# S5 input side by pairs of tiles, thinner scan steps and a shorter way to the output side in a two-layer encoder kernel

## The chip, the cores and the metric

The kernel runs on one core of one Trainium2 chip. The metric is the device time of one execution in microseconds (us), as the median of several runs. All data are fp32, and all weights lie in HBM when the program starts.

Engines are called as in the profile: PE is TensorE's matmul, PEld its weight load, DVE VectorE, ACT ScalarE, POOL GpSimd, SP SyncE (it issues most of the DMAs; SPq is its queue). An `x16` behind an instruction in the trace is a count of records. A matmul of plain fp32 operands leaves two records, so eight such instructions are `x16`; the transposes (a matmul against the identity) and the matmuls on fp32r operands leave one.

## The reference

A sequence of 256 frames of width 2048 passes two layers. Each has its own modulation from a conditioning vector, a mixer on a width of 4096, and a residual with LayerNorm. Layer 0 is a gated linear attention, layer 1 a state-space model (S5):

```
mod = silu(c) @ ada_w + ada_b                  # shift, scale, gate per layer
u   = x * (1 + scale) + shift
h   = gla_mixer(u)  or  s5_mixer(u)
x   = layer_norm(alpha * x + (1 + gate) * h)

def s5_mixer(u_in):
    u, z = split(u_in @ w_in)                  # 2048 -> 4096 + 4096
    # per group of 16 channels, 64 complex states, 256 groups:
    x_t = lambda * x_{t-1} + B u_t             # lambda = exp(dt * a)
    y_t = Re(C x_t) + d * u_t
    y   = gelu(y)
    y   = y * sigmoid(y @ w_glu + b_glu)       # 4096 x 4096
    return (y * silu(z)) @ w_out               # 4096 -> 2048
```

## The kernel before, in words

**Weight streams.** Nearly all the time goes into products with large fp32 weights. A weight is read in tiles of 128x1024, which hold two blocks of 128 rows (`kp` counts such pairs) and 512 columns (a group `g`). `wload` (L133) loads one; its buffer comes from `ring`, a list of buffers that is used in rotation: four of the pool `w`, and, while a phase has memory to spare, some of the phase's own pool, which are put at the head of the list. `split` makes two fp32r tiles of it: `hi`, a cast on ACT (L109), and `lo`, the weight minus `hi`, on DVE (L110). There are three buffers for each. PE then makes three products, hi x hi, hi x lo, lo x hi: `st_step` (L168 to L170) has 24 matmuls of 128x256 per weight tile, into four PSUM banks of the pool `mm` (five banks). Another PSUM pool, `ax`, has three banks and serves all that is not a weight stream.

**The S5 layer** runs in this order: `su`, 8 groups of 8 tiles, the input projection u; `sz`, 8 groups, the gate z; `gl`, the 4096x4096 GLU product; `op`, the output projection. In the trace of before su runs from 777.2 to 1052.3 us, sz to 1324.8, gl to 1692. The state-space model is computed beside su and sz, in pieces that are put between two weight tiles. Its 256 groups of channels are handled as 32 tiles `f` of 8 groups; one su group yields four tiles.

**Input side, beside su and the first group of sz.** Time is cut in blocks of 8 frames. For a tile, `b_pow` builds B times powers of lambda, `wb` (one copy on ACT, three operations on DVE, from `rb`, loaded for two tiles at a time), `b_tr` transposes it (pswb, two banks one after the other, each copied to `wbt` by ACT), `s_in` turns u into blocks (a DVE transpose to `vv`, two PE transposes psu, an ACT copy to `U`; it stands behind the last matmul of the group). `s_mm` multiplies: 8 instructions `pss<-wbt,U`, whose result is transposed on DVE into the block states `sx`, and 8 instructions `pss<-wb,rb`, whose result is copied to `kT` on ACT. `k_out` transposes kT (psk), copies it to `ks` on ACT, adds d on the diagonal (`dm` and `ks` on DVE) and writes it to DRAM (`dk`). These pieces stand in the list `bq`; `bstep` takes as many as `b_pace` has run up, 1.5 per weight tile.

**The scan.** `scan` advances the state from block to block, 30 steps for each half of the channels, four small DVE operations a step. The first half is put into the list `bg` behind su's group 4, and `pump` takes `SCAN_RATE` pieces per weight tile.

**Output side, beside sz groups 1 to 7.** When sz's group 0 is done, what is left of `bq` and `bg` is issued, the phase's pool is closed, and another one is opened in the same memory. Per tile `cside` loads `cl` (three DMAs) and `mt` (the matrices from `dk`) and builds C times powers (`wc0`, `wc1`, in `powmul`, L970 and L971, double-buffered); for tiles with f % 8 >= 5 DVE adds the two (L1109). `xstage` transposes the states (xT on DVE, psxs on PE, xS on ACT), and `ystage` multiplies: `psy<-mt,U` and `psy<-wc,xS`, once for each wc. The second half of the scan, three steps per tile, runs in the same list, and `pump` takes 2.311 pieces per weight tile.

**What sets the order.** The program is written in the order in which these lists are emptied. A scheduler then orders each engine's instructions; pools with few buffers add waits. Each engine works in its own order, and waits on semaphores of the others.

Of the kernel before, what the change touches and what calls it, by code (L numbers as in the profile page):

```python
# [8 lines left out]
F32 = mybir.dt.float32  # L9
# [24 lines left out]
def trunk(ctx, tc, x, c, ln_g, ln_b, ada_w, ada_b, gla_w_in, gla_gate_w2, gla_gate_b, gla_norm_g,  # L34
# [33 lines left out]
    rp.open("rows0")  # L68
    tp = Phase()
# [13 lines left out]
    ones = cp.tile([P, P], F32, name="ones")  # L83
    V.memset(ones, 1.0)
# [18 lines left out]

    last_lo = [None]

    def split(w, name):
        hi = hp.tile([P, 1024], F32R, tag="hi", name="hi" + name)
        lo = lp.tile([P, 1024], F32R, tag="lo", name="lo" + name)
# [5 lines left out]
    ring = [lambda name: wp.tile([P, 1024], F32, tag="w", name=name)] * 4  # L114

    def ring_add(bufs):
        ring[0:0] = bufs

    def ring_tmp(n):
        bufs = [lambda name: tp.tile([P, 1024], F32, tag="wx", name=name, bufs=n)] * n  # L120
        ring_add(bufs)
        return bufs[0]

    def ring_drop(buf):
        ring[:] = [b for b in ring if b is not buf]

    def wload(src, k0, c0, name, last=False):
        if last:
            w = wp.tile([P, 1024], F32, tag="w", name="w" + name)
        else:  # L130
            ring.append(ring.pop(0))
            w = ring[-1]("w" + name)
        dma(w.rearrange("p (k c) -> p k c", k=2),  # L133
            src[k0 * P:(k0 + 2) * P, c0:c0 + 512].rearrange("(k p) c -> p k c", p=P))
        return w

    def split_last(w, name, i):


        hi = (hp.tile([P, 1024], F32R, tag="hi", name="hi" + name) if i % 2 else lp.tile([P, 1024], F32R, tag="lo", name="hi" + name))  # L140
# [256 lines left out]
    early = ring_tmp(2)  # L397
# [9 lines left out]
    l8r = cp.tile([P, 128], F32, name="l8r")  # L407
    l8i = cp.tile([P, 2, 128], F32, name="l8i")
# [32 lines left out]
    def prep_lambda():  # L441
# [301 lines left out]
    ring_drop(early)  # L743
    tp.close()
    tp.open("tmp0b")
    mid = ring_tmp(4)
# [154 lines left out]
    ring_add(spare)  # L901
# [19 lines left out]
    ring_drop(mid)  # L921
    for b in spare:
        ring_drop(b)
# [49 lines left out]
    wu, kts = {}, {}  # L973

    def b_pow(f):
        if f % 2 == 0:
            bload(f // 2)
        a = rb[f // 2][:, f % 2]

        w = tp.tile([P, 8, 16, 8], F32, tag="wu", name=f"wb{f}", bufs=2)  # L980
# [8 lines left out]
        wu[f] = w  # L989

    def b_tr(f):
        wt = tp.tile([P, 8, 128], F32, tag="wbt", name=f"wbt{f}", bufs=2)
        for h in range(2):
            ps = psx(f"pswb{f}{h}")
            for g in range(4):
                PE.transpose(ps[:, g * P:(g + 1) * P], wu[f][:, 4 * h + g].rearrange("p i s -> p (i s)"), ident)
            S.copy(wt[:, 4 * h:4 * h + 4, :], ps.rearrange("p (g r) -> p g r", g=4))
        wb[f] = wt

    def s_in(f, ps):  # L1000
        v = tp.tile([P, 2, 16, 8], F32, tag="vv", name=f"vv{f}", bufs=2)
        V.transpose(v.rearrange("p b i s -> p s b i"), ps[:, :T].rearrange("p (s b i) -> p s b i", s=8, b=2)[:, ::-1])
        pu = psx(f"psu{f}")
        for b in range(2):
            PE.transpose(pu[:, b * P:(b + 1) * P], v[:, b].rearrange("p i s -> p (i s)"), ident)
        U = Ut[f // 8][:, f % 8]
        S.copy(U, pu[:, :T].rearrange("p (b r) -> p b r", b=2))

    def s_mm(f):
        U = Ut[f // 8][:, f % 8]  # L1010
        pss = psx(f"pss{f}")
        for b in range(2):
# [17 lines left out]
    def k_out(f):  # L1030
        kt_ = kts[f]
        pk_ = psx(f"psk{f}")
        for b in range(2):
            PE.transpose(pk_[:, b * P:(b + 1) * P], kt_[:, b], ident)
        pk = pk_[:, :T].rearrange("p (b q i) -> p q b i", b=2, q=4)[:, :, :, :16]
        ks = tp.tile([P, P], F32, tag="ks", name=f"ks{f}", bufs=1)
        S.copy(ks.rearrange("p (q b i) -> p q b i", q=4, b=2), pk)
        dm = tp.tile([16, 8, 16], F32, tag="dm", name=f"dm{f}", bufs=1)
        V.tensor_tensor(dm, ident[:16, :16].unsqueeze(1).to_broadcast([16, 8, 16]),
                        dT[:, 8 * f:8 * f + 8].unsqueeze(2).to_broadcast([16, 8, 16]), op=ALU.mult)  # L1040
        V.tensor_tensor(ks[:16].rearrange("p (q b i) -> p q b i", q=4, b=2), pk[:16],
                        dm.rearrange("p (q b) i -> p q b i", q=4), op=ALU.add)
        kd = dk[16 * f:16 * f + 16, 896:1920].rearrange("i (n c) -> n i c", n=8)
        wdma(kd, ks)
# [285 lines left out]
```

## Time and profile before

| what | us |
|---|---|
| median of 3 runs | 1884.14 |
| lowest and highest run | 1879.79, 1885.82 |
| the profiled execution's own time | 1875.77 |
| its span | 1874.0 |
| PE busy | 1811.6 (97%), 13443 instructions |
| PE weight load busy | 1582.1 (84%) |
| DVE busy | 1441.9 (77%), 2022 instructions |
| ACT busy | 899.1 (48%) |
| POOL busy | 26.9 (1%), 44 instructions |

The mean granted clock of the profiled execution is 0.993. Matmuls are pipelined, so a record's duration (0.28 us for 128x256) is longer than the distance from one start to the next. Costs of PE work are read from the starts. The busy shares are means over stages, so a stage's limit is read from the windows.

### The profile page before, as it was taken

How to read it: one execution, taken by the hardware profiler on the slowest of the kernel's cores; microseconds unless marked ns; L12 is line 12 of the kernel's file. 1: busy time of each engine (PE TensorE's matmuls, PEld its weight loads, DVE VectorE, ACT ScalarE, POOL GpSimd, SP SyncE). 2: the span in 40 equal slices, each digit the busy share in tenths (PEclk: the TensorE clock that was granted, in tenths of full speed). 3: DMA queues.
4: the chain of work that ended last, by engine and by line, in shares of the span. 5: the costliest groups of instructions: out<-in, count | busy, mean ns of one | idle time of the engine just before them, and what ended most of it. 6: DMA issues, size and time to landing. Idle time of an engine off the chain costs nothing.

```text
span 1874.0 us, 33634 instructions
## 1 busy us (share of the span) xinstructions
PE 1811.6 (97%) x13443; PEld 1582.1 (84%) x13443; DVE 1441.9 (77%) x2022; ACT 899.1 (48%) x1259; POOL 26.9 (1%) x44
## 2 busy tenths in 40 slices
PE   6999999999999999999999999999899999999997
PEld 3786797899999888898899889898788888888886
DVE  2787675989999888687799879998767775557556
ACT  3533365655556333654454444554544444444332
POOL 0000000000000000000000000000000000000000
PEclk9999999999999999999999999999999999999999
DMA  9978976789888998564555567898678887668653
GB/s 357 321 256 264 354 246 183 230 284 326 287 290 311 342 346 275 168 178 146 165 154 143 167 202 209 221 255 235 212 250 269 270 267 226 190 190 326 192 172 109
DMA packets 239493, 449.12 MB, mean 240 GB/s; under 512 B 19221, under 2 KB 45263, under 8 KB 238055
## 3 DMA queue, kind: packets, MB, share of 16 engines
q1 hardware_dynamic: 235400, 437.53, 73.2%
q0 software_dynamic: 3168, 8.41, 1.4%
q8 instruction: 105, 1.72, 0.4%
q10 hardware_dynamic: 768, 1.05, 0.2%
q14 instruction: 52, 0.42, 0.1%
HBM read 432.49 MB, written 14.42 MB: 238 GB/s over the span
## 4 chain that ended last, share of the span: by engine, by line
PE 64%; issue 9%; DVE 6%; DMA 6%; ACT 1%; POOL 1%; SPq 0%; DVEq 0%; POOLq 0%; ACTq 0%
PE gl L180 13%; PE gl L181 6%; PE op L157 5%; PE op L155 5%; PE op L156 5%; PE z L170 3%; PE z L168 3%; PE z L169 3%; PE su L168 2%; PE su L170 2%; PE su L169 2%; DMA cl<-rec 2%; PE sz L168 2%; PE sz L170 2%; PE sz L169 2%
## 5 line engine op out<-in xcount | busy, mean ns | idle before, releaser
L110 DVE TENSOR_TENSOR logl<-wgl,higl 128x1024 fp32r<-128x1024 f32 x128 | 156.6, 1224 | 118.7 <-ACT higl L109 113.4
L109 ACT CAST higl<-wgl 128x1024 fp32r<-128x1024 f32 x128 | 134.2, 1050 | 177.9 <-PE gl L180 174.6
L180 PE MATMUL gl<-yp,higl 128*128 128x512 f32 x512 | 181.2, 399 | 3.1 <-ACT higl L109 3.1
L180 PE MATMUL gl<-yb,higl 128*128 128x512 f32 x512 | 178.7, 394 | 0.0
L109 ACT CAST hio<-wo 128x1024 fp32r<-128x1024 f32 x96 | 101.3, 1055 | 155.6 <-PE op L157 131.1
L110 DVE TENSOR_TENSOR loo<-wo,hio 128x1024 fp32r<-128x1024 f32 x96 | 117.3, 1224 | 65.6 <-ACT hio L109 63.6
L280 DVE SCALAR_TENSOR_TENSOR acc<-wa,cs,acc 128x512 f32<-128x512 f32 x215 | 160.7, 747 | 4.0 <-DMA wa<-in_ada_w 1.3
L170 PE MATMUL sz<-u1h,losz 128*128 128x256 f32 x512 | 146.5, 287 | 3.9 <-DVE losz L110 3.9
L168 PE MATMUL sz<-u1h,hisz 128*128 128x256 f32 x512 | 149.8, 293 | 0.2 <-ACT zs L1166 0.2
L168 PE MATMUL su<-u1h,hisu 128*128 128x256 f32 x512 | 149.8, 294 | 0.0
L168 PE MATMUL z<-u0h,hiz 128*128 128x256 f32 x512 | 148.7, 290 | 0.9 <-ACT hiz L109 0.9
L170 PE MATMUL su<-u1h,losu 128*128 128x256 f32 x512 | 147.7, 290 | 0.0
L169 PE MATMUL su<-u1l,hisu 128*128 128x256 f32 x512 | 147.1, 287 | 0.0
L170 PE MATMUL z<-u0h,loz 128*128 128x256 f32 x512 | 145.1, 283 | 1.7 <-DVE loz L110 1.7
L169 PE MATMUL sz<-u1l,hisz 128*128 128x256 f32 x512 | 145.5, 284 | 0.0
L169 PE MATMUL z<-u0l,hiz 128*128 128x256 f32 x512 | 144.7, 283 | 0.0
L181 PE MATMUL gl<-yb,logl 128*128 128x256 f32 x512 | 142.7, 279 | 0.0
L181 PE MATMUL gl<-yp,logl 128*128 128x256 f32 x512 | 141.7, 279 | 0.1
L180 PEld LDWEIGHTS gl<-yp,higl 128*128 128x128 f32 x512 | 95.9, 188 | 27.0 <-ACT higl L109 3.3
L180 PEld LDWEIGHTS gl<-yb,higl 128*128 128x128 f32 x512 | 96.0, 187 | 22.4
L155 PE MATMUL v<-hiv,u0h 128*128 128x512 f32 x256 | 103.3, 410 | 5.2 <-ACT u0h L309 2.6
L109 ACT CAST hiz<-wz 128x1024 fp32r<-128x1024 f32 x64 | 67.1, 1053 | 83.8 <-PE z L169 78.4
(319 smaller groups left out, 4965.8 us busy)
## 6 DMA issues: line engine op xcount, KB each, us to landing
wgl<-in_s_w_glu SPq DMA_DIRECT2D x128, 512.0 KB, 4.7
wa<-in_ada_w SPq DMA_DIRECT2D x115, 512.0 KB, 5.1
a<-in_ada_w SPq DMA_DIRECT2D x32, 1024.0 KB, 11.4
wv<-in_gla_w_in SPq DMA_DIRECT2D x64, 512.0 KB, 6.1
wz<-in_gla_w_in SPq DMA_DIRECT2D x64, 512.0 KB, 5.1
wsu<-in_s_w_in SPq DMA_DIRECT2D x64, 512.0 KB, 3.9
wsz<-in_s_w_in SPq DMA_DIRECT2D x64, 512.0 KB, 5.3
wo<-in_s_w_out SPq DMA_DIRECT2D x64, 512.0 KB, 4.6
```

The costliest lines, as they stand in the source:

```text
L109: S.copy(hi, w)
L110: last_lo[0] = V.tensor_tensor(lo, w, hi.bitcast(F32), op=ALU.subtract).ins
L155: PE.matmul(banks[tt], lhsT=uh, rhs=hi[:, kk, :], start=(k == first), stop=False)
L156: PE.matmul(banks[tt], lhsT=uh, rhs=lo[:, kk, :], start=False, stop=False)
L157: PE.matmul(banks[tt], lhsT=ul, rhs=hi[:, kk, :], start=False, stop=(k == last))
L168: PE.matmul(o, lhsT=wh, rhs=u.hi(k), start=(k == first), stop=False)
L169: PE.matmul(o, lhsT=wh, rhs=u.lo(k), start=False, stop=False)
L170: PE.matmul(o, lhsT=wl, rhs=u.hi(k), start=False, stop=(k == last))
L180: PE.matmul(banks[f], lhsT=hi[:, kk, fs], rhs=u.both(k), start=(k == 0), stop=False)
L181: PE.matmul(banks[f][:, :T], lhsT=lo[:, kk, fs], rhs=u.hi(k), start=False, stop=(k == last))
L280: V.scalar_tensor_tensor(acc[0], w[:, kk, :], cs[:, k:k + 1], acc[0], op0=ALU.mult, op1=ALU.add)
```

## The change

It has six parts.

1. Buffers. `ring` becomes a class, with one ring each for w, hi and lo. Buffers of a phase are appended (used last) where they were put at the head. During su, from its tile (0, 3) on, there is one more w, one more hi and one more lo.
2. Input side by pairs of tiles. u's transposes (psu) of a pair are issued from weight tiles 0 and 3 of the next group, four PE transposes in a row into one bank. `s_mm(p)` has the 32 instructions of two tiles in one piece, in two banks; kT, ks and dm hold a pair each, one buffer. dm and the add to ks go to POOL. `wb` and `wbt` are pairs in the pool `s8`. `b_pace` is 1.0 per weight tile.
3. Scan. Two multiplications become one of twice the size, against a constant `l8` of another layout; four operations become three. `SCAN_RATE` is 1.25.
4. The DVE add of wc0 and wc1 goes; all tiles multiply both.
5. The output side is opened at sz's tile (0, 5), where it was opened behind (0, 7). Two scan steps per tile, not three, and they stand between `cside` and `xstage`. `Y_RATE` is 2.25, and `zs` is allocated group by group.
6. `ones` lies in the phase pool `rows` and not among the constants.

The core of the diff (`b_pow` and `b_tr` change only in that they write into the pair tiles; `...` marks what is left out):

```diff
+    class Ring(list):
+        def take(self, name):
+            self.append(self.pop(0))
+            return self[-1](name)
...
+        def add_tmp(self, tag, dt, n):
+            bufs = [lambda name: tp.tile([P, 1024], dt, tag=tag, name=name, bufs=n)] * n
+            self.extend(bufs)
+            return bufs[0]
-    def ring_add(bufs):
-        ring[0:0] = bufs
...
-    def s_mm(f):
-        U = Ut[f // 8][:, f % 8]
-        pss = psx(f"pss{f}")
...
-        kt_ = tp.tile([P, 2, P], F32, tag="kt", name=f"kT{f}", bufs=2)
+    def s_in2(p, v):
+        pu = psx(f"psu{p}")
+        for i in range(2):
+            for b in range(2):
+                PE.transpose(pu[:, (2 * i + b) * P:(2 * i + b + 1) * P], v[:, i, b].rearrange("p i s -> p (i s)"), ident)
...
+    def s_mm(p):
+        pss = [psx(f"pss{2 * p + i}") for i in range(2)]
+        for i in range(2):
...
+            for b in range(2):
+                for q in range(4):
+                    PE.matmul(pss[i][32 * q:32 * q + 32, b * P:(b + 1) * P], lhsT=U[:, b, 32 * q:32 * q + 32],
+                              rhs=wb[p][:, i, 2 * q + b, :], start=True, stop=True)
+            for b in range(2):
+                for q in range(4):
...
+        kt_ = tp.tile([P, 2, 2, P], F32, tag="kt", name=f"kT{p}", bufs=1)
...
-        dm = tp.tile([16, 8, 16], F32, tag="dm", name=f"dm{f}", bufs=1)
-        V.tensor_tensor(dm, ident[:16, :16].unsqueeze(1).to_broadcast([16, 8, 16]),
...
+        dm = tp.tile([16, 16, 16], F32, tag="dm", name=f"dm{p}", bufs=1)
+        nc.gpsimd.tensor_tensor(dm, ident[:16, :16].unsqueeze(1).to_broadcast([16, 16, 16]),
...
+        nc.gpsimd.tensor_tensor(kv, kv, dm.rearrange("p g i -> p (g i)"), op=ALU.add)
+        for i in range(2):
+            f = 2 * p + i
+            wdma(dk[16 * f:16 * f + 16, 896:1920].rearrange("i (n c) -> n i c", n=8), ks[:, i])
...
-    for f in range(35):
-        if 2 <= f < 34:
-            bq.append(lambda f=f: s_mm(f - 2))
-        if f < 32:
-            bq.append(lambda f=f: (b_pow(f), b_tr(f)))
-        if f >= 3:
-            bq.append(lambda f=f: k_out(f - 3))
+    for p in range(18):
+        if 1 <= p < 17:
+            bq.append(lambda p=p: s_mm(p - 1))
+        for f in (2 * p, 2 * p + 1):
+            if f < 32:
+                bq.append(lambda f=f: (b_pow(f), b_tr(f)))
+        if p >= 2:
+            bq.append(lambda p=p: k_out(p - 2))
...
-        V.tensor_tensor(t1, X, lr.unsqueeze(1).to_broadcast([P, 2, 2, 32]), op=ALU.mult)
-        V.tensor_tensor(t2, X[:, ::-1], li, op=ALU.mult)
-        V.tensor_tensor(t1, t1, t2, op=ALU.add)
-        V.tensor_tensor(N, N, t1, op=ALU.add)
+        V.tensor_tensor(t1, X.unsqueeze(1).to_broadcast([P, 2, 2, 64]), l8[:, h], op=ALU.mult)
+        V.tensor_tensor(t1[:, 0], t1[:, 0], t1[:, 1, ::-1], op=ALU.add)
+        V.tensor_tensor(N, N, t1[:, 0], op=ALU.add)
...
+            if us and kp in (0, 3):
+                us.pop(0)()
+            if (g, kp) == (0, 3):
+                mid = more(1, 1)
...
-        for i in range(4):
-            s_in(4 * g + i, banks[i])
+        for i in range(2):
+            v = s_in(2 * g + i, banks[2 * i:2 * i + 2])
+            us.append(lambda p=2 * g + i, v=v: s_in2(p, v))
...
-        if f % 8 >= SPLIT:
-            V.tensor_tensor(w[0], w[0], w[1], op=ALU.add)
-            w.pop()
...
+    def output_side():
+        bstep(len(bq))
+        while bg:
+            bg.pop(0)()
+        less(mid)
+        tp.close()
+        tp.open("tmp2")
+        sc1 = [lambda cidx=cidx: scan(cidx, 1) for cidx in range(1, 31)]
+        for f in range(34):
+            if f < 32:
+                bg.append(lambda f=f: cside(f))
+            for _ in range(2):
...
+            pump(SCAN_RATE if (g, kp) < (0, 6) else Y_RATE)
+            if (g, kp) == (0, 5):
+                output_side()
```

How the order moves is seen best in the queues themselves. The first place is PE in su's group 3, where tiles 8 and 9 are multiplied. A row gives the line, the operation, out<-in by name, and the size; the digits behind su are group and bank, and those behind pss and wbt the tile, or, after the change, the pair for wbt. Here is the kernel before, for the second tile of the pair alone:

```order
L170 MATMUL su33_8762<-u1h0_7394,losu32_8878 128x256
L1014 MATMUL pss9_8905<-wbt9_8713,U1_7519 32x128 x8
L168 MATMUL su30_8759<-u1h0_7394,hisu33_8927 128x256
L169 MATMUL su30_8759<-u1l0_7396,hisu33_8927 128x256
L170 MATMUL su30_8759<-u1h0_7394,losu33_8928 128x256
L168 MATMUL su30_8759<-u1h0_7394,hisu33_8927 128x256
L169 MATMUL su30_8759<-u1l0_7396,hisu33_8927 128x256
L1024 MATMUL pss9_8905<-wb9_8707,rb4_8595 32x128 x8
L170 MATMUL su30_8759<-u1h0_7394,losu33_8928 128x256
```

And the same place after the change, with both tiles:

```order
L182 MATMUL su33_8681<-u1h0_7394,losu31_8734 128x256
L1038 MATMUL pss8_8761<-wbt4_8612,U1_7519 32x128 x8
L1043 MATMUL pss8_8761<-wb4_8606,rb4_8602 32x128 x8
L1038 MATMUL pss9_8762<-wbt4_8612,U1_7519 32x128 x8
L1043 MATMUL pss9_8762<-wb4_8606,rb4_8602 32x128 x8
L180 MATMUL su30_8678<-u1h0_7394,hisu32_8802 128x256
```

Before, the two halves of a tile stood five su matmuls apart, and tile 8 had its own two pieces some 48 matmuls earlier. Now the four pieces of a pair stand between two su matmuls.

The second place is PE where wb of tile 10 is transposed. Before:

```order
L169 MATMUL su30_8759<-u1l0_7396,hisu32_8877 128x256
L996 MATMUL pswb100_8854<-ident_87,wb10_8847 128x128 x4
L996 MATMUL pswb101_8860<-ident_87,wb10_8847 128x128 x4
L1034 MATMUL psk7_8866<-ident_87,kT7_8675 128x128 x2
L170 MATMUL su30_8759<-u1h0_7394,losu32_8878 128x256
```

After the change the halves of wb (pswb100 and pswb101) are apart:

```order
L1010 MATMUL pswb100_8841<-ident_89,wb5_8834 128x128 x4
L180 MATMUL su30_8678<-u1h0_7394,hisu33_8855 128x256
L181 MATMUL su30_8678<-u1l0_7396,hisu33_8855 128x256
L182 MATMUL su30_8678<-u1h0_7394,losu33_8856 128x256
L180 MATMUL su30_8678<-u1h0_7394,hisu33_8855 128x256
L181 MATMUL su30_8678<-u1l0_7396,hisu33_8855 128x256
L182 MATMUL su30_8678<-u1h0_7394,losu33_8856 128x256
L180 MATMUL su31_8679<-u1h0_7394,hisu33_8855 128x256
L181 MATMUL su31_8679<-u1l0_7396,hisu33_8855 128x256
L182 MATMUL su31_8679<-u1h0_7394,losu33_8856 128x256
L1010 MATMUL pswb101_8847<-ident_89,wb5_8834 128x128 x4
```

Three pieces that stood in a row, each in a bank of its own, are now put nine su matmuls apart, as psu and psk are from them.

The third place is DVE in sz, around tiles 22 to 25 of the output side (wc0 and wc1 carry the tile's number behind the 0 or 1, as wc023 and wc123; losz carries group and weight tile). Before:

```order
L1147 STREAM_TRANSPOSE yt20_14115<-psy20_14090 128x256
L1109 TENSOR_TENSOR wc022_14048<-wc022_14048,wc122_14049 128x1024
L971 TENSOR_TENSOR wc123_14125<-cl23_14118 128x1024
L970 TENSOR_TENSOR wc023_14124<-cl23_14118 128x1024
L1147 STREAM_TRANSPOSE yt21_14183<-psy21_14166 128x256
L1109 TENSOR_TENSOR wc023_14124<-wc023_14124,wc123_14125 128x1024
L971 TENSOR_TENSOR wc124_14193<-cl24_14186 128x1024
L1126 STREAM_TRANSPOSE xT23_14226<-sx_7515 128x256
L110 TENSOR_TENSOR losz65_14303<-wsz65_14300,hisz65_14302 128x1024
L971 TENSOR_TENSOR wc125_14290<-cl25_14283 128x1024
```

After:

```order
L1154 STREAM_TRANSPOSE xT23_13946<-sx_7515 128x256
L146 TENSOR_TENSOR losz63_13984<-wsz63_13981,hisz63_13983 128x1024
L981 TENSOR_TENSOR wc023_13837<-cl23_13831 128x1024
L982 TENSOR_TENSOR wc123_13838<-cl23_13831 128x1024
L1175 STREAM_TRANSPOSE yt21_13903<-psy21_13878 128x256
L146 TENSOR_TENSOR losz64_14031<-wsz64_14028,hisz64_14030 128x1024
L1154 STREAM_TRANSPOSE xT24_14021<-sx_7515 128x256
L146 TENSOR_TENSOR losz65_14099<-wsz65_14096,hisz65_14098 128x1024
L981 TENSOR_TENSOR wc024_13942<-cl24_13936 128x1024
L982 TENSOR_TENSOR wc124_13943<-cl24_13936 128x1024
```

Before, wc124 stands ahead of xT23 and losz65. After the change xT24 stands ahead of wc024 and wc124, the two readers of a cl stand side by side, and losz has its place between the tiles.

## Rows read from the trace of the kernel before

**Rows 1.** Windows: su, its scan stretch, sz, and ten us of sz.

```profile
core 0: us, PE busy (x) PEld busy (x) DVE busy (x) ACT busy (x) POOL busy (x), PEclk, DMA share, GB/s
777.20:1052.30 275.10, 272.47 (x2796) 249.17 (x2795) 235.93 (x402) 141.94 (x262) 15.51 (x26) 0.99 0.55 160
946.90:1052.10 105.20, 104.71 (x1105) 94.84 (x1104) 103.62 (x229) 52.52 (x96) 7.14 (x12) 1.00 0.54 157
...
1087.20:1324.80 237.60, 220.26 (x2756) 206.68 (x2753) 217.50 (x332) 118.26 (x184) 0.82 (x2) 0.99 0.83 227
1100.00:1110.00 10.00, 6.94 (x48) 6.74 (x48) 9.18 (x19) 1.51 (x4) 0.00 (x0) 0.83 0.87 248
```

**Rows 2.** PE's waits, whole run: waited for, us in total, times, longest.

```profile
PE psxs L1129 <- DVE xT L1126: 8.8, 3, 3.9
...
PE sz L170 <- DVE losz L110: 3.9, 4, 3.1
...
PE gl L180 <- ACT higl L109: 3.1, 1, 3.1
...
PE psu L1005 <- DVE vv L1002: 2.0, 4, 0.6
```

**Rows 3.** PE's timeline in su: start, duration, engine, line, operation, out<-in.

```profile
906.65 0.28 PE L169 MATMUL su<-u1l,hisu 128*128 128x256 f32 x1
906.77 0.28 PE L170 MATMUL su<-u1h,losu 128*128 128x256 f32 x1
906.98 0.65 PE L1014 MATMUL pss<-wbt,U 128*32 128x128 f32 x16
907.55 0.39 PE L168 MATMUL su<-u1h,hisu 128*128 128x256 f32 x1
907.78 0.28 PE L169 MATMUL su<-u1l,hisu 128*128 128x256 f32 x1
```

**Rows 4.** PE's timeline in sz, one run of 16 records in psy.

```profile
1112.72 0.62 PE L1144 MATMUL psy<-wc,xS 128*32 128x128 f32 x16
1113.15 0.40 PE L1141 MATMUL psy<-mt,U 128*32 128x128 f32 x8
```

**Rows 5.** PE's timeline in su around two of u's transposes.

```profile
913.74 0.28 PE L169 MATMUL su<-u1l,hisu 128*128 128x256 f32 x1
...
913.85 0.41 PE L1005 MATMUL psu<-ident,vv 128*128 128x128 f32 x2
...
914.02 0.36 PE L170 MATMUL su<-u1h,losu 128*128 128x256 f32 x1
```

**Rows 6.** PE's timeline in su, eight of wb's transposes and what follows.

```profile
912.06 1.04 PE L996 MATMUL pswb<-ident,wb 128*128 128x128 f32 x8
...
912.94 0.38 PE L1034 MATMUL psk<-ident,kT 128*128 128x128 f32 x2
```

**Rows 7.** DVE's groups in sz: count, busy us, mean ns, idle before.

```profile
L1109 DVE TENSOR_TENSOR wc<-wc,wc 128x1024 f32<-128x1024 f32 x12 | 14.3, 1188 | 0.0
```

**Rows 8.** DVE's waits, 740 to 1325 us.

```profile
DVE wc L971 <- DMA cl<-rec: 9.1, 5, 3.7
```

**Rows 9.** Timeline in sz: a load of cl and its reader.

```profile
1263.54 0.34 SPq L1099 DMA_DIRECT2D cl<-rec  x1
...
1266.87 1.22 DVE L971 TENSOR_TENSOR wc<-cl 128x1024 f32<-128x1024 f32 x1 [1.90 <-DMA cl<-rec]
```

**Rows 10.** Timelines of ACT and SP at the start of the output side.

```profile
1091.12 0.27 ACT L1037 COPY ks<-psk 128x128 f32<-128x128 f32 x1 [2.40 <-DMA dk<-ks]
...
1094.56 0.34 SPq L1099 DMA_DIRECT2D cl<-rec  x1
```

**Rows 11.** ACT's groups, 810 to 1090 us.

```profile
L109 ACT CAST hisu<-wsu 128x1024 fp32r<-128x1024 f32 x53 | 55.6, 1050 | 66.6 <-issue 36.9 <-PE su L169 28.5 <-ACT wb L981 1.2
L997 ACT COPY wbt<-pswb 128x512 f32<-128x512 f32 x60 | 32.2, 589 | 9.7 <-PE pswb L996 9.5
```

**Rows 12.** DVE's groups in the scan stretch, 946.9 to 1052.1 us.

```profile
L1070 DVE TENSOR_TENSOR sca<-sx,l8r 128x128 f32<-128x128 f32 x30 | 8.2, 273 | 0.0
...
L1041 DVE TENSOR_TENSOR ks<-psk,dm 16x128 f32<-16x128 f32 x12 | 3.3, 274 | 0.0
```

More of the change, by code (lines that the diff above doesn't have):

```diff
@@ L68, in trunk @@
     rp.open("rows0")
+    ones = rp.tile([P, P], F32, tag="ones", name="ones0")
+    V.memset(ones, 1.0)
     tp = Phase()
@@ L101, in pump, with drop, more, less @@
                 bg.pop(0)()
+    class Ring(list):
+        def take(self, name):
+            self.append(self.pop(0))
+            return self[-1](name)
+        def drop(self, buf):
+            self[:] = [b for b in self if b is not buf]
+        def add_tmp(self, tag, dt, n):
+            bufs = [lambda name: tp.tile([P, 1024], dt, tag=tag, name=name, bufs=n)] * n
+            self.extend(bufs)
+            return bufs[0]
+    ring = Ring([lambda name: wp.tile([P, 1024], F32, tag="w", name=name)] * 4)
+    his = Ring([lambda name: hp.tile([P, 1024], F32R, tag="hi", name=name)] * 3)
+    los = Ring([lambda name: lp.tile([P, 1024], F32R, tag="lo", name=name)] * 3)
+    def more(nw, nh):
+        got = [(ring, ring.add_tmp("wx", F32, nw))]
+        for r, tag in ((his, "hx"), (los, "lx")):
+            if nh:
+                got.append((r, r.add_tmp(tag, F32R, nh)))
+        return got
+    def less(got):
+        for r, b in got:
+            r.drop(b)
+    def wload(src, k0, c0, name, last=False):
+        w = wp.tile([P, 1024], F32, tag="w", name="w" + name) if last else ring.take("w" + name)
+        dma(w.rearrange("p (k c) -> p k c", k=2),
+            src[k0 * P:(k0 + 2) * P, c0:c0 + 512].rearrange("(k p) c -> p k c", p=P))
+        return w
     last_lo = [None]
     def split(w, name):
-        hi = hp.tile([P, 1024], F32R, tag="hi", name="hi" + name)
-        lo = lp.tile([P, 1024], F32R, tag="lo", name="lo" + name)
+        hi = his.take("hi" + name)
+        lo = los.take("lo" + name)
         S.copy(hi, w)
@@ L111, in split @@
         return hi.rearrange("p (k c) -> p k c", k=2), lo.rearrange("p (k c) -> p k c", k=2)
-    ring = [lambda name: wp.tile([P, 1024], F32, tag="w", name=name)] * 4
-    def ring_add(bufs):
-        ring[0:0] = bufs
[L119 to L135, printed above, removed]
     def split_last(w, name, i):
-        hi = (hp.tile([P, 1024], F32R, tag="hi", name="hi" + name) if i % 2 else lp.tile([P, 1024], F32R, tag="lo", name="hi" + name))
+        hi = (his if i % 2 else los).take("hi" + name)
         lo = (tp.tile([P, 1024], F32R, tag="wx", name="lo" + name, bufs=4) if i < 4 else
@@ L742, in trunk @@
     qs.append(qt[:, :, 192:256])
-    ring_drop(early)
+    less(early)
     tp.close()
     tp.open("tmp0b")
-    mid = ring_tmp(4)
+    mid = more(4, 0)
     sts = s8t("sts", [4, 384])
@@ L920, in trunk @@
         pump()
-    ring_drop(mid)
+    less(mid)
     for b in spare:
-        ring_drop(b)
+        ring.drop(b)
     ab1 = cp.tile([P, 2, 16], F32, name="ab1")
@@ L988, in b_pow @@
         V.tensor_tensor(w[:, :, :, 1:8], w[:, :, :, 1:8], t_, op=ALU.subtract)
-        wu[f] = w
     def b_tr(f):
-        wt = tp.tile([P, 8, 128], F32, tag="wbt", name=f"wbt{f}", bufs=2)
+        p = f // 2
+        if f % 2 == 0:
+            wb[p] = s8t(f"wbt{p}", [2, 8, 128])
         for h in range(2):
@@ L1030, in k_out @@
[L1030 to L1037, printed above, removed]
-        dm = tp.tile([16, 8, 16], F32, tag="dm", name=f"dm{f}", bufs=1)
-        V.tensor_tensor(dm, ident[:16, :16].unsqueeze(1).to_broadcast([16, 8, 16]),
[L1040 to L1044, printed above, removed]
@@ new lines, in k_out @@
+    def k_out(p):
+        kt_ = kts[p]
+        pk_ = psx(f"psk{p}")
+        for i in range(2):
+            for b in range(2):
+                PE.transpose(pk_[:, (2 * i + b) * P:(2 * i + b + 1) * P], kt_[:, i, b], ident)
+        ks = tp.tile([P, 2, P], F32, tag="ks", name=f"ks{p}", bufs=1)
+        for i in range(2):
+            S.copy(ks[:, i].rearrange("p (q b i) -> p q b i", q=4, b=2),
+                   pk_[:, i * T:(i + 1) * T].rearrange("p (b q i) -> p q b i", b=2, q=4)[:, :, :, :16])
+        dm = tp.tile([16, 16, 16], F32, tag="dm", name=f"dm{p}", bufs=1)
+        nc.gpsimd.tensor_tensor(dm, ident[:16, :16].unsqueeze(1).to_broadcast([16, 16, 16]),
+                                dT[:, 16 * p:16 * p + 16].unsqueeze(2).to_broadcast([16, 16, 16]), op=ALU.mult)
+        kv = ks[:16].rearrange("p f c -> p (f c)")
+        nc.gpsimd.tensor_tensor(kv, kv, dm.rearrange("p g i -> p (g i)"), op=ALU.add)
+        for i in range(2):
+            f = 2 * p + i
+            wdma(dk[16 * f:16 * f + 16, 896:1920].rearrange("i (n c) -> n i c", n=8), ks[:, i])
@@ L1188, in trunk @@
     rp.open("rows1")
+    ones = rp.tile([P, P], F32, tag="ones", name="ones1")
+    V.memset(ones, 1.0)
     tp.open("tmp3")
-    ring_tmp(4)
+    more(4, 0)
     yb = bigp.tile([P, 8448], F32R, tag="big", name="yb")
```

124 lines of the change are left out of this document (54 added, 70 removed).

## The prediction

> **What bounds the kernel now.** I went from the windows by stage to PE's waits, then into PE's timeline at two places where it leaves a weight stream, then to DVE. The windows [rows 1] show TensorE under matmuls almost without a break in the input groups (su): 272.47 of 275.10 us. Only the gate stage (sz, 1087.2 to 1324.8) has a hole, 220.26 of 237.60. So time can leave in three ways alone: fewer or cheaper PE records, stalls that go, and a clock that doesn't drop behind them. PE's waits [rows 2] name the stalls in reach: xT 8.8 us in three, losz 3.9 in four, vv 2.0 in four, and higl 3.1 at the start of GLU. The second thing to see in the windows is DVE: in 946.9 to 1052.1, where the scans run, it is busy 103.62 of 105.20 us. There it stands as near the end as PE.
>
> **A. One s_mm for a pair.** PE's timeline [rows 3] shows what it costs to leave the su stream for 16 small records and come back. From the start at 906.77 to that at 907.78 pass 1.01 us, in which two su matmuls at the pitch of 0.12 (906.65 to 906.77) take 0.24: the excursion costs 0.77. Its slope is small: in sz 16 records of the same form, 128x32 weights on 128x128, take from 1112.72 to 1113.15, 0.43 us, 0.027 each [rows 4]. So 0.43 of the 0.77 is work and 0.34 the going and coming. Before, each tile goes twice, a pair four times: 4 x 0.77 = 3.08. The changed kernel issues the 64 records of a pair in one piece: 0.34 + 64 x 0.027 = 2.07. That is 1.01 less per pair, -16 for 16 pairs. Lower bound: if a record here costs 0.57/16 = 0.036 (906.98 to 907.55), the piece costs 0.34 + 2.30 = 2.64, and the sum is -7. Upper bound -16.3 (three turns of 0.34, 16 times), since the records themselves stay. The transposes, which the change cuts into more pieces, carry no such price: two of psu between su at 913.74 and su at 914.02 take 0.28 - 0.12 = 0.16, or 0.08 each [rows 5], no more than in a long run (8 in 0.88, from 912.06 to 912.94 [rows 6]). So four separate pswb cost nothing for being separate.
>
> **B. u's transposes later.** The wait for vv arises because psu stands right behind the DVE transpose of a bank just finished. One tile into the next group 24 su matmuls, 2.9 us, lie between, more than a lo and two transposes queued on DVE: -2. The bound is 0, where DVE's queue is as late as PE.
>
> **C. SPLIT gone.** Twelve tiles no longer add their two halves on DVE (12 x 1188 ns = 14.3 us [rows 7]); PE multiplies both, 96 instructions, 192 records x 0.027 = +5.2. They lengthen stretches that exist, so no going is added. By 0.036 it is +6.9.
>
> **D. The gate stage.** DVE waits 9.1 us for cl in five waits [rows 8]. The timeline [rows 9] shows one: a cl load goes out at 1263.54, when its buffer is free, and DVE starts its wc at 1266.87, 3.3 us later. Behind that wc stand xT and losz, and PE waits for xT (3.9 at the most). The granted clock falls after a stall: 0.83 in 1100 to 1110 [rows 1], which is 1.7 us of matmul; for the other two I add 1.3, an estimate. What can go is 8.8 + 3.9 + 3 = 15.7. In the changed order both wc of a tile stand together, xT stands ahead of its own tile's wc and not behind the next tile's, and no add keeps a reader of cl waiting; two scans instead of three lie between tiles, and DVE has 14.3 us less to do. Against it: the first stall stands at the start of the output side, where ks of the last k_out (1091.12) and its DMA come ahead of the first cl load at 1094.56 [rows 10]. The new kernel opens that stage two tiles sooner, but the chain of ACT copy, POOL add, two DMAs and landing is no shorter. I leave 3.7 there: -12. Bounds -15.7, and -2 where the stalls only move.
>
> **E. New buffers last.** higl's 3.1 us is GLU's first tile waiting for a buffer of a pool just opened; the changed ring hands out an old one. The first load and cast remain: -2, between 0 and -3.1.
>
> **F. What the pair costs in PSUM.** kT is one buffer, so ACT's copy of pair p waits until psk of p-1 was read, and both banks of s_mm stay held until then. Of three ax banks one is left: four pswb, psu and psk pass through it in turn, each after ACT has emptied it. ACT's copy takes 589 ns [rows 11]; with the last transpose's 0.27 (it starts 7 x 0.11 after 912.06 and ends 1.04 after it [rows 6]) and some 0.09 for the hand-overs it is 0.95 from the last transpose to the next. The su matmuls between two turns are 9 (1.08 us) or 15, and once per pair 6 (0.72): 0.23 uncovered, and more where a hi cast, 1050 ns, has gone ahead of the copy. I take 0.3 per pair, +5. Bounds 0 and one whole cast per pair, 16.8.
>
> **G. DVE while the scans run.** A scan has three operations for four; two of 128x128 (273 ns) give way to one twice as wide, for which there is no row here: 0 to 0.27 saved, 30 times 0 to 8, I take 4, the middle. ks and dm, of one size, leave DVE: 2 x 12 x 274 = 6.6 [rows 12]. 103.62 - 10.6 = 93.0, and PE's stretch shrinks by six pairs x 1.01 to some 99. DVE's slack grows from 1.6 to some 6, which isn't room enough to be free of waits: +2.5, bounds 0 and 6.6 (the saving doesn't arrive).
>
> Costed at nothing: l8's four multiplications on ACT in place of two copies (ACT is half idle in every window), ones in another pool, zs allocated late, a fourth hi and lo in su (more lead, DMA share 0.55). Uncovered, each is a few tenths.
>
> **Sum** on the profiled execution: -16 - 2 + 5.2 - 12 - 2 + 5 + 2.5 = -19.3, from 1875.77 to some 1856. That execution lies 8.4 under the median of 1884.14, so the forecast is 1884.14 - 19.3 = 1865.
>
> **Rivals.** R1, the other side: the one free PSUM bank. If a cast is ahead of the copy at three turns of a pair, 3 x 1.05 x 16 = 50 us are lost in place of 5: -24.3 + 50 = +26, 1910. It decides from 24.3/16 = 1.5 us per pair. For it: ACT has 1.05 of cast in every 2.9 us and works in order. Against: with a fourth hi a cast is not urgent and may stand behind the copy. R2: little arrives. The records cost 0.036 (A -7, C +6.9) and the gate's stalls move (D -2): -7 - 2 + 6.9 - 2 - 2 + 5 + 2.5 = +1.4, 1885.5. For it: DVE is busy 217.50 of 237.60 in sz, and cl still has two buffers, refilled when the reader is done. Against: 14.3 us leave DVE there. R3: every stall goes, F and G cost nothing: -16 - 2 + 5.2 - 15.7 - 3.1 = -31.6, 1852.5. For it the half idle ACT, against it the last k_out. R4: POOL's operations hold DVE up as long as those they replace took, 6.6 us, all in the stretch without slack: -19.3 + 6.6 = -12.7, 1871.4. Against: nothing of before shows POOL slowing DVE, its work there being DMA issues.
>
> [...]
>
> **How the numbers follow.** Forecast (1857 to 1868) 0.46; R3 0.14; R4, and what lies between it and R2, 0.18; R2 0.11; R1 0.11. Less than 0.3% (5.7 us) either way a measurement of this kernel can't tell from no change. Faster: the first three, 0.78; same: R2, 0.11; slower: R1, 0.11. The range goes from 1847, inside R3, to 1882, short of R2, and leaves out R1, most of R2 and the end of R3, 2 in 10; the likeliest case alone has 1857 to 1868.
>
> **What would show it.** A: pss in one run of 64 records, 2.0 to 2.2 us between su and su, an su group some 2 us shorter. B: no wait on vv. C: 16 records of psy more in tiles 5 to 7 of each eight, 0.43 us longer. D: no PE wait on xT but one of some 3.7 near the start of the output side; a granted clock of 1.00 after it. F: PE's idle time behind wbt in su; over 1.5 us per pair R1 holds. G: DVE's share in the scan stretch below 0.97; lengthened DVE operations beside POOL's would show R4. The forecast is wrong if PE's waits in su add up to over 10 us, if xT's wait stays over 6, or if a piece of 64 costs over 2.6.

## The result and the profile after

The changed kernel took 1864.34 us in the median of 5 runs (1861.98 to 1871.52), the kernel before 1885.82 beside it (1879.79 to 1889.19). The ratio is 0.9894 with the interval [0.9865, 0.9923]: 20 us less, between 14.5 and 25.5. The forecast was 1865 in a range of 1847 to 1882.

The profiled execution of the changed kernel took 1861.99 us, 13.8 less than the one of before (1875.77). So the profile of before caught a quick execution, and a second one was taken (the ninth experiment), which took 1882.56. The changed kernel's profile is the second quickest of its five runs. The table gives the stages by the start of their first matmul.

| stage, us | before, first profile | before, second profile | after |
|---|---|---|---|
| start of su | 777.17 | 776.24 | 775.59 |
| su | 275.17 | 276.41 | 273.14 |
| sz group 0 | 34.85 | 34.75 | 32.84 |
| sz groups 1 to 7, to GLU's first matmul | 237.57 | 244.03 | 228.91 |
| from there to the end of the execution | 551.01 | 551.13 | 551.51 |

The windows of the changed kernel, for su, its scan stretch, and sz groups 1 to 7 (columns as in [rows 1]):

```profile
core 0: us, PE busy (x) PEld busy (x) DVE busy (x) ACT busy (x) POOL busy (x), PEclk, DMA share, GB/s
775.60:1048.70 273.10, 263.14 (x2795) 250.63 (x2794) 235.42 (x324) 136.18 (x248) 48.03 (x49) 0.99 0.56 169
943.00:1048.50 105.50, 98.02 (x1071) 92.76 (x1070) 100.30 (x159) 47.60 (x90) 27.36 (x24) 0.98 0.53 158
1081.50:1310.50 229.00, 221.94 (x2948) 209.48 (x2947) 208.07 (x292) 118.03 (x183) 0.50 (x1) 1.00 0.88 236
```

The hole has moved: sz has 7 us without a matmul where it had 17 [rows 1], and su has 10 where it had under 3. POOL is busy 48 us in su, three times as long as before. PE's waits of the changed kernel say which holes these are:

```profile
PE psu L1025 <- ACT wbt L1011: 6.9, 5, 2.4
...
PE sz L182 <- DVE losz L146: 3.0, 2, 1.7
PE psxs L1157 <- DVE xT L1154: 2.9, 3, 1.1
...
PE pswb L1010 <- ACT wbt L1011: 2.3, 2, 1.4
```

xT has gone from 8.8 to 2.9, and vv and higl from the list [rows 2]. New is 9.2 us behind wbt. One of these seven places, in the timelines of SP, ACT and PE of the changed kernel:

```profile
986.41 0.37 SPq L136 DMA_DIRECT2D wsu<-in_s_w_in  x1
986.87 0.42 SPq L968 DMA_DIRECT2D rb<-rec  x1
987.35 1.24 SPq L970 DMA_DIRECT2D rb<-rec  x2
...
987.53 0.58 ACT L1011 COPY wbt<-pswb 128x512 f32<-128x512 f32 x1
991.82 0.66 ACT L994 COPY wb<-rb 128x128 f32<-128x128 f32 x2 [3.71 <-DMA rb<-rec]
992.28 0.62 ACT L1011 COPY wbt<-pswb 128x512 f32<-128x512 f32 x1
...
992.96 0.55 PE L1025 MATMUL psu<-ident,vv 128*128 128x128 f32 x3 [2.35 <-ACT wbt L1011]
```

ACT stands 3.71 us at the copy of the next pair's wb, because rb has not landed. The second wbt copy, which has its data, stands behind it, and psu needs the bank that this copy empties. The first line is a weight load, which stands ahead of the rb load in SP's queue; the third experiment comes back to it. ACT's waits for rb, with before's first and the changed kernel's second:

```profile
ACT wb L981 <- DMA rb<-rec: 1.4, 1, 1.4
```

```profile
ACT wb L994 <- DMA rb<-rec: 22.8, 9, 3.7
```

The piece of s_mm is what was forecast: 64 records in 2.10 us, from 981.42 to 983.52.

```profile
981.42 0.28 PE L182 MATMUL su<-u1h,losu 128*128 128x256 f32 x1
981.63 0.64 PE L1038 MATMUL pss<-wbt,U 128*32 128x128 f32 x16
982.09 0.62 PE L1043 MATMUL pss<-wb,rb 128*32 128x128 f32 x16
982.53 0.62 PE L1038 MATMUL pss<-wbt,U 128*32 128x128 f32 x16
982.97 0.62 PE L1043 MATMUL pss<-wb,rb 128*32 128x128 f32 x16
983.52 0.39 PE L180 MATMUL su<-u1h,hisu 128*128 128x256 f32 x1
```

### The profile page after: what moved, and what is told of

Its sections match the earlier page's. It is cut to its first block, busy times and chain, and to the rows that moved or that the text cites. A ratio compares the mean times of both kernels' runs of the same rounds, so it can differ in the third digit from the quotient of the medians.

```text
span 1860.2 us, 33837 instructions
## 1 busy us (share of the span) xinstructions
PE 1804.7 (97%) x13635; PEld 1588.6 (85%) x13635; DVE 1422.9 (76%) x1886; ACT 890.5 (48%) x1245; POOL 67.4 (4%) x76
## 3 DMA queue, kind: packets, MB, share of 16 engines
q10 hardware_dynamic: 768, 1.05, 0.2%
## 4 chain that ended last, share of the span: by engine, by line
PE 69%; DVE 7%; DMA 6%; ACT 2%; issue 1%; SPq 0%; POOL 0%; DVEq 0%; ACTq 0%; POOLq 0%
PE gl L192 13%; PE gl L193 6%; PE op L168 5%; PE op L169 5%; PE op L167 5%; PE z L182 3%; PE z L180 3%; PE z L181 3%; PE sz L180 3%; DMA rb<-rec 2%; PE sz L182 2%; PE sz L181 2%; PE su L180 2%; PE su L181 2%; PE su L182 2%
```

## The experiments

All edits are to the changed kernel (1864.34), unless the text says otherwise. Ratios are to the kernel before, run beside each, in 4 to 12 runs. Only for the sixth and the twelfth experiment does the interval lie clear of the changed kernel's [0.9865, 0.9923]; for the others the difference in time is a hint, and the reading rests on the waits and costs in the traces.

**A third rb buffer.** The extra w of su goes, for memory.

```diff
-        a = tp.tile([P, 2, 512], F32, tag="rb", name=f"rb{f2}", bufs=2)
+        a = tp.tile([P, 2, 512], F32, tag="rb", name=f"rb{f2}", bufs=3)
...
-                mid = more(1, 1)
+                mid = more(0, 1)
```

> The changed kernel with a third buffer for rb (the loads of B's tables for a pair), and for memory without the extra w buffer in su. In the trace of the changed kernel PE stands 9.2 us behind wbt in seven places of su and the start of sz, and in the five of them looked at ACT's copy of wb from rb waits for the rb load just ahead of the wbt copy. Theory 1 (the late rb load holds up ACT's in-order queue): the 9.2 us fall below 1.5, the rb waits of ACT below 3 us in all, and the time falls by 5 to 9 us, to some 1857. Rival (the single free PSUM bank behind hi casts): PE's waits on wbt stay near 9 us, time within 3 us of 1864 or above it for the missing w buffer.

1858.58 us, 0.9866 [0.9842, 0.989]. No PE wait on wbt is left, and ACT's waits for rb are down to one:

```profile
ACT wb L994 <- DMA rb<-rec: 1.7, 1, 1.7
```

su took 264.85 us in place of 273.14. Theory 1 holds: the late load is the cause. From the issue of a load to ACT's first copy from it pass, from the third load on, 17 us or more here, in the changed kernel as little as 4.4, in the kernel before 7.9 or more. The extra w, which went with the same edit, isn't the reason: the twelfth experiment has it, and no wait on wbt either. Of these 8.3 us the profiled execution lost 5 again in sz groups 1 to 7: 3.2 as idle time (xT 4.6 for 2.9, and some small ones), 2.0 as longer matmuls, at a granted clock of 0.993 for 1.000.

**kT in three single buffers.**

```diff
-        kt_ = tp.tile([P, 2, 2, P], F32, tag="kt", name=f"kT{p}", bufs=1)
+        kt_ = [tp.tile([P, 2, P], F32, tag="kt", name=f"kT{2 * p + i}", bufs=3) for i in range(2)]
...
```

> The changed kernel with kT by single tiles in three buffers in place of one buffer for a pair (1 KB more), so that one of the two banks of s_mm is free as soon as ACT copies it. Theory (the bank is what chains psu to the late wbt copy): PE's waits on wbt fall from 9.2 to under 4 us, because psu or the next pswb finds another bank, and the time falls by 4 to 7 us. Rival (ACT late, whatever the banks): waits on wbt between 7 and 10 us, time within 2 us of 1864.

1863.65 us, 0.9902 [0.9877, 0.9927]. The waits on wbt are gone, but eight like them, 8.4 us, stand behind U and kT, and ACT still waits 20.6 us for rb. With another bank the stall has only another name; the rival is right on the time.

**dm and the add on DVE.**

```diff
-        nc.gpsimd.tensor_tensor(dm, ident[:16, :16]...
+        V.tensor_tensor(dm, ident[:16, :16]...
-        nc.gpsimd.tensor_tensor(kv, kv, dm...
+        V.tensor_tensor(kv, kv, dm...
```

> The changed kernel with dm and the add to ks on DVE again, as whole pairs (16x256), in place of POOL. Theory (POOL's operations lengthen the DVE operation beside them by about 0.5 us each, but PE does not wait for DVE there): the lengthened DVE operations (1.62 and 1.63 for 1.08, 1.10 for 0.64) go back to their short values, DVE has 32 operations of 0.3 to 0.4 us more, and the time stays within 2 us of 1864. [...]

1859.43 us, 0.9873 [0.9846, 0.99]. The changed kernel's timelines of POOL and DVE show the collision:

```profile
1017.13 1.49 POOL L1068 TENSOR_TENSOR ks<-ks,dm 16x256 f32<-16x256 f32 x1 [11.35 <-ACT ks L1062]
1020.16 0.89 POOL L1065 TENSOR_TENSOR dm<-ident,dT 16x256 f32<-16x256 f32 x1
```

```profile
1016.95 2.62 DVE L999 TENSOR_TENSOR wb<-rb 128x896 f32<-128x896 f32 x2
1019.50 1.08 DVE L1001 TENSOR_TENSOR wb<-wb,pt 128x896 f32<-128x896 f32 x1
1020.50 1.64 DVE L146 TENSOR_TENSOR losu<-wsu,hisu 128x1024 fp32r<-128x1024 f32 x1
```

The pair of operations at 1016.95 takes 2.62 us, where the same pair takes 2.06 at 873.91 without a neighbour on POOL, and the lo at 1020.50 takes 1.64, where the one at 985.17 takes 1.21. POOL's own operations take 0.61 us (dm) and 0.73 (the add) where DVE is idle, and up to 4.22 beside it. DVE's transposes from PSUM aren't lengthened beside POOL: no single one takes over 0.70 us here, and the 1.10 of the expectation is the length of two in one row. With both on DVE (the add 0.41 us, and dm 0.40 in the twelfth experiment's kernel) the lo and wb's last operation take 1.21 and 1.07 us in the mean, where the changed kernel's scan stretch has 1.24 and 1.13:

```profile
L146 DVE TENSOR_TENSOR losu<-wsu,hisu 128x1024 fp32r<-128x1024 f32 x20 | 24.1, 1206 | 0.0
...
L1001 DVE TENSOR_TENSOR wb<-wb,pt 128x896 f32<-128x896 f32 x12 | 12.9, 1074 | 0.0
```

The median fell by 4.9 (4.0 by the ratios), more than the theory's 2 and less than R4's 6.6; the intervals of the two kernels overlap, but su of the profiled execution is 4.9 shorter too (268.27). PE's waits don't name DVE: what shrank are the waits on wbt (9.2 to 4.4) and ACT's on rb (22.8 to 12.6).

One way from DVE to rb stands in the changed kernel's trace. The rb load at 986.87 has had its buffer free since 983.6, the end of the s_mm piece above. But in SP's queue the weight load of 986.41 stands ahead of it, and SP waits 5.4 us there, until DVE's lo has read the weight buffer, at 986.38. So whatever makes DVE late makes this rb load late; of the 3.3 us, a lengthened operation ahead of the lo (0.70 us for 0.29) is 0.4:

```profile
984.55 0.70 DVE L1097 TENSOR_TENSOR sca<-sca 128x128 f32<-128x128 f32 x1
985.17 1.21 DVE L146 TENSOR_TENSOR losu<-wsu,hisu 128x1024 fp32r<-128x1024 f32 x1
```

From the last pss record that reads a buffer to the load that fills it again pass, for 14 loads, 18.8 us in the changed kernel, 12.1 with both operations on DVE, and 4.7 in the kernel before, where no weight load came between. So DVE is on the way to rb without PE waiting for it. It is a part only: in the fourth experiment these 14 times add up to 6.4 us, and ACT still waits 19.7 us for rb.

**s_mm in three pieces.** Pieces of 32, 16 and 16 records with six su matmuls between them: `st_step` takes the later ones from a list, one per bank.

```diff
         for f in range(4):
+            if late:
+                late.pop(0)()
```

> The changed kernel with s_mm of a pair in three pieces (32, 16 and 16 records) with six su matmuls between two pieces, all else kept. Two more goings and comings per pair. By the prediction's 0.34 each: +0.68 per pair, +10.9 in all, 1875; by the gaps of the two traces (0.88 less per pair for three fewer, 0.29 each) +9.4. Rival (a record costs 0.036 and the going 0.1): +3, 1867.

1872.29 us, 0.9941 [0.9918, 0.9963]: +8.0. One of the pieces in PE's timeline of this kernel:

```profile
918.21 0.28 PE L186 MATMUL su<-u1h,losu 128*128 128x256 f32 x1
918.42 0.65 PE L1043 MATMUL pss<-wbt,U 128*32 128x128 f32 x16
919.00 0.39 PE L184 MATMUL su<-u1h,hisu 128*128 128x256 f32 x1
919.22 0.28 PE L185 MATMUL su<-u1l,hisu 128*128 128x256 f32 x1
```

From 918.21 to 919.22 the 1.01 us of [rows 3] are back. Over su groups 2 to 6 the pss records with the su matmul behind them cost, beyond the pitch of 0.12 and without waits, 5.47 us a group where the changed kernel has 4.15. A group has four goings more: 0.33 each, where the prediction had 0.34.

**SPLIT back.**

```diff
+        if f % 8 >= 5:
+            V.tensor_tensor(w[0], w[0], w[1], op=ALU.add)
+            w.pop()
```

> The changed kernel with the old DVE add of wc0 and wc1 for the tiles with f % 8 >= 5, so with 192 psy records fewer on PE and 14.3 us more on DVE in sz. Theory (PE gains the 192 x 0.027 = 5.2 us that the change spent, but DVE, busy 208.57 of 229.50 us in sz groups 1 to 7 of the changed kernel, has no room for 14.3 more, so stalls behind xT, losz and cl come back): PE's waits in sz rise from 7.0 us to 12 or more, time between 1863 and 1869. Rival (DVE has the room; the change's stalls went by the order alone): waits in sz stay near 7, time 1859.

1869.16 us, 0.9928 [0.9909, 0.9948]: +4.8. PE's waits in sz:

```profile
PE sz L182 <- DVE losz L146: 7.7, 4, 4.2
PE psxs L1160 <- DVE xT L1157: 5.7, 5, 2.9
PE psy L1172 <- DMA mt<-dk: 0.5, 2, 0.3
```

13.9 us against 6.7. The theory holds, though the time lies 0.2 above its range: the 5 us of PE work that the change adds buy about 10.

**New buffers first.**

```diff
-            self.extend(bufs)
+            self[0:0] = bufs
```

> The changed kernel with a phase's new buffers put at the head of the rings again, as before the change. Theory (the first weight tiles of z and GLU wait for a pool only just opened): PE waits again about 3 us at the start of GLU and 1 to 2 at the start of z, time 3 to 5 us more, 1868. Rival (the gap at GLU's start went for another reason, the shorter sz): no PE wait on higl over 1 us, time within 2 us of 1864.

1882.61 us, 0.9991 [0.9976, 1.0007]. The whole gain is gone, and both theories are wrong by far:

```profile
PE su L180 <- ACT hisu L145: 9.2, 1, 9.2
PE gl L192 <- ACT higl L145: 1.4, 1, 1.4
PE z L180 <- ACT hiz L145: 0.5, 1, 0.5
```

GLU starts 1.6 us later behind the last sz matmul, and z's waits are 1.3 longer. The 9.2 are the fifth weight tile of su, the first that takes su's own extra buffers, which the kernel before did not have: su's start is 12 us longer. So "used last" is worth some 3 us against before, and it is also what makes extra buffers in su harmless.

**Output side opened behind (0, 7).**

```diff
-            if (g, kp) == (0, 5):
-                output_side()
...
+        if g == 0:
+            output_side()
```

> The changed kernel with the output side opened behind sz's tile (0, 7) again, all else kept (two scan steps per tile, cside first). Theory (two tiles' time, 5.8 us, is given to the last k_out and the first loads in which PE has sz matmuls either way; what the later opening costs is the pieces pushed to the end): PE's waits in sz change by less than 2 us, the end of sz has up to 3 us more of psy without sz matmuls, time 1864 to 1868. Rival (the early opening is what took the xT stalls away): an xT or losz wait of 3 us returns, time 1870 or more.

1867.77 us, 0.9919 [0.9899, 0.9938]: +3.4, in the theory's range. But the waits grew by more than the theory's 2 us: an xT wait of 4.1 us is back, near the end of sz, as the rival had it, and GLU starts 5.5 us behind the last sz matmul. Neither holds whole:

```profile
PE psxs L1157 <- DVE xT L1154: 6.1, 2, 4.1
PE psy L1169 <- DMA mt<-dk: 2.2, 1, 2.2
```

**Third rb buffer, and dm and the add on DVE.** The two edits above together.

> The changed kernel with both edits that gained: three rb buffers for the extra w buffer, and dm and the add to ks on DVE. Theory (two separate costs: the rb load ahead of wbt in ACT's order, and POOL's operations that hold up DVE and, through it, the pairs): the gains of 5.8 and 4.9 add up in part, since DVE alone took the waits on wbt from 9.2 to 4.5 and the rb buffers all of them: 1855 to 1857. Rival (one cost seen twice): 1858 to 1860. No PE wait on wbt over 1 us in either case.

1856.16 us, 0.9854 [0.9831, 0.9877], with no wait on wbt. That the gains add up in part fits, but the 2.4 us under the first experiment lie inside the intervals. From su group 1 to its end PE has no wait at all, and su takes 262.18 us.

**The kernel before once more.**

> The kernel before once more, unchanged, for a second profile. Its first profiled execution took 1875.77 us, at the low end of the timed ones (1875.76 to 1889.63, median 1883.2). Theory (the executions differ in the stalls of sz, which hang on DMA landings): an execution of 1880 to 1888 us, whose su is within 1 us of the first one's 275.2 and whose sz is longer. Rival (the clock or the start differ): the stage lengths grow all alike.

1882.56 us. Its su is 1.2 us longer than the first one's, its sz groups 1 to 7 6.5 us longer, the rest is the same within 1 us. In the windows of this execution:

```profile
776.20:1052.70 276.50, 273.02 (x2797) 249.67 (x2796) 236.14 (x402) 141.92 (x262) 15.51 (x26) 0.99 0.54 160
1087.20:1331.40 244.20, 224.02 (x2756) 210.28 (x2755) 218.14 (x331) 119.05 (x184) 1.04 (x2) 0.97 0.81 220
```

Its granted clock in sz is 0.97, where the first has 0.99, and PE waits for xT 8.7, losz 4.1, mt 4.0 and higl 3.0. Of the 6.5 us, 2.9 are idle time, mostly behind mt, and 3.6 longer matmuls at the lower clock. Both are of the kind that the change takes away: its sz has 7 us of idle time and a clock of 1.00.

**Four operations a scan step.** The multiplication of 128x256 as two of 128x128.

```diff
-        V.tensor_tensor(t1, X.unsqueeze(1).to_broadcast([P, 2, 2, 64]), l8[:, h], op=ALU.mult)
+        for j in range(2):
+            V.tensor_tensor(t1[:, j], X, l8[:, h, j], op=ALU.mult)
```

> The changed kernel with the one 128x256 multiplication of a scan step as two of 128x128, so four DVE operations a step as before. Theory (in the changed kernel PE does not wait for DVE in su but for the rb load, so DVE's 30 x 0.12 us in su are covered): time within 2 us of 1864. Rival (DVE is the limit while the scans run): 3 to 5 us more, 1868, with PE waits on losu or vv in su groups 5 to 7.

1863.81 us, 0.9887 [0.987, 0.9905]. The thinner step is worth nothing that can be measured here: theory held.

**No extra hi and lo in su.**

```diff
-                mid = more(1, 1)
+                mid = more(1, 0)
```

> The changed kernel without the extra hi and lo buffer in su, three of each as before; the extra w stays. Theory (the fourth pair is what keeps casts out of the way of wbt and lets lo run ahead of the scans): PE's waits in su rise from 8.5 us to 12 or more, time 1868 to 1872. Rival (the lead is not used, PE's waits come from rb alone): within 2 us of 1864.

1861.19 us, 0.9875 [0.9856, 0.9895]. The theory falls: PE's idle time in su is 8.3 us, no more than the changed kernel's 10. The time is even 1 us under the rival's range; the fourth pair brings nothing.

**Third rb buffer, dm and the add on DVE, extra w, no extra hi and lo.**

> The changed kernel with three rb buffers, with dm and the add to ks on DVE, with the extra w buffer in su and without the extra hi and lo. Theory (the extra hi and lo bring nothing, as their removal alone showed, and one w more gives a little lead): 1854 to 1858, no PE wait on wbt over 1 us. Rival (with the rb wait gone the extra hi and lo are what gives lead): 1859 or more, with PE waits on lo or vv in su.

1852.23 us (1848.9 to 1856.04), 0.9827 [0.9811, 0.9843]: by the ratio 32.6 us under the kernel before (29.6 to 35.6), and 12 under the changed one. That is 2 us under the theory's range, and no run says which of the edits gave them. In the windows of su and of sz groups 1 to 7, PE has no hole left in su:

```profile
776.00:1040.00 264.00, 263.26 (x2802) 250.13 (x2802) 236.72 (x349) 138.20 (x250) 14.27 (x24) 0.99 0.57 173
1073.20:1304.40 231.20, 224.42 (x2947) 212.25 (x2946) 207.39 (x292) 118.16 (x183) 0.00 (x0) 0.99 0.88 232
```

## Why the prediction came out right, step by step

The time is within 1 us of the forecast, but the sum was made against the first profile, against which the change gained 13.8 and not 19.3. Against the second, which lies near the median of before, it gained 20.6. What each step measured, against the first and the second profile, is in the table. Waits are the idle times in PE's timeline; records of pss, psy and the transposes are counted from start to start of the stream's matmuls around them, less 0.12 for each. For pss and the transposes the slowed su matmul behind them is counted in, the price is that of su groups 2 to 6, and it is taken for all 16 pairs.

| step | forecast | first | second |
|---|---|---|---|
| A, s_mm in one piece | -16 | -16.8 | -16.8 |
| A, transposes in more pieces | 0 | +6.2 | +6.2 |
| B, F, G, PE's waits in su and sz group 0 | +5.5 | +7.5 | +6.8 |
| C, psy | +5.2 | +4.0 | +3.5 |
| D, waits and slow matmuls in sz | -12 | -9.4 | -15.3 |
| E, starts of z and GLU | -2 | -4.6 | -3.7 |
| sum | -19.3 | -13.1 | -19.3 |

That the second column hits the forecast is luck: its terms miss by up to 6 us, and the misses cancel.

**A** had the right mechanism and the right size for s_mm: a going of 16 records costs 0.78 us, the piece of 64 costs 2.08 where 2.07 was forecast, and a pair saves 1.05 for 1.01. (The lower bound of 7 was too careful: if a record costs 0.036, the going is 0.20 and not 0.34, and the sum is -9.) The step that failed is "four separate pswb cost nothing for being separate". A run of four in the changed kernel, PE's timeline:

```profile
986.38 0.28 PE L182 MATMUL su<-u1h,losu 128*128 128x256 f32 x1
986.50 0.60 PE L1010 MATMUL pswb<-ident,wb 128*128 128x128 f32 x4
986.85 0.36 PE L180 MATMUL su<-u1h,hisu 128*128 128x256 f32 x1
987.05 0.28 PE L181 MATMUL su<-u1l,hisu 128*128 128x256 f32 x1
```

From 986.38 to 987.05 pass 0.67 us, 0.43 beyond two pitches; four at 0.08 had been 0.32. The 0.08 itself was read short: [rows 5] stop at the su matmul behind the transposes, where the reading of pss went one su matmul further. In PE's timeline of the kernel before that one is slowed too, 0.20 for 0.12:

```profile
914.22 0.28 PE L168 MATMUL su<-u1h,hisu 128*128 128x256 f32 x1
```

So the two psu cost 0.24 and not 0.16. Counted like this, a group's transposes cost 5.69 us before, in 7 runs, and 6.47 after, in 12: 0.16 for each run more. That is why a su group became only 0.5 us shorter and not the 2 of the prediction's sign: 2.1 less for pss, 0.8 more for the transposes, 0.8 more of waits.

**B and F.** The waits on vv went as forecast. F was right in size (a wait of 9.9 in all in su and sz group 0 where it had been 2.4) and wrong in cause: it named a hi cast in ACT's queue, and it is the copy that waits for rb, as the first experiment shows. The prediction read the bank and ACT's order correctly and didn't ask which instruction in that order waits for a DMA; [rows 11] show none, because before only one copy had waited. DVE's waits of before, in the window of [rows 8], had a sign that rb came without much to spare:

```profile
DVE pt L987 <- DMA rb<-rec: 3.3, 7, 1.0
```

The idle time in su, 9.96 us, is just short of the 10 that the prediction had as a sign of being wrong.

**G and R4.** DVE is still the busiest engine beside PE in the scan stretch (100.30 of 105.50, 0.95), but PE doesn't wait for it there. The share is under the 0.97 that was its sign. The thinner scan is worth nothing that can be measured (tenth experiment), and of the 6.6 us of dm and ks some 5.2 came back as lengthened operations: so much longer are DVE's large groups here, by their means, than with both on DVE (third experiment). The lo at 1020.50 has it, 1.64 us beside POOL for 1.21. An undisturbed operation of POOL takes 0.73 us here for the add and 0.61 for dm. R4's sign came, but the time is the forecast's and not R4's 1871.4. What POOL costs, 4 to 5 us, is not clear of the noise; one way by which it arrives goes from DVE over SP's queue to rb (third experiment), and how much of it goes there isn't shown.

**C and D.** C was forecast as a price alone; the fifth experiment shows that it is paid back twice, since the waits of sz come from DVE's load. D's bounds (-15.7 and -2) hold both profiles. The fifth and the seventh experiment show DVE's load and the early opening as parts of it; the new order of xT and wc and the two scan steps per tile were not taken back alone, so their share isn't shown. The wait of 3.7 us that was to stay at the start of the output side is two, 1.7 behind losz and 0.8 behind xT.

**E** was mis-sized: GLU's wait went altogether, and z's waits fell from 2.6 us (2.2 in the second profile) to 0.9. **R1** didn't come: 9.9 us in 16 pairs are 0.6 per pair, with 1.5 needed. **R2** and **R3** lie outside of what was measured.

## What to carry to other kernels

Leaving a weight stream for small records on a quarter of the columns costs a fixed 0.33 to 0.35 us here, and for transposes 0.16, so such pieces belong together; but look at what else is split up in exchange, and read the price of both the same way, to the second matmul behind. When a step is merged, ask for each load in it how long before its use its buffer comes free, which loads stand ahead of it in its queue, and which ready instructions stand behind the first one that needs it. A profile of one execution may be the quick one: two profiles show which terms of a sum vary.

## What the hardware showed unexpectedly

POOL's two-input operations of 16x256 took 0.61 and 0.73 us alone and up to 4.22 beside two-input DVE operations, and the last two-input DVE operation that began while one ran took 0.4 to 0.6 us more (1.08 to 1.63, 0.29 to 0.70). Those that began earlier weren't longer: beside the 4.22 at 962.62, a wb operation at 963.49 took 1.08 and the lo at 964.70 took 1.22. Moving them off DVE gave DVE's time back only in small part: some 5.2 of 6.6 us came back in longer operations.
